# A two-block fp32 transformer kernel: row factors on ScalarE, a norm's scale and bias moved behind its mix, a 64-row matmul widened, first loads reordered

## The chip, the cores and the metric

The kernel runs on one core of one Trainium2 chip. The metric is the time on the device in microseconds, the median of three runs. A profile is one execution of its own, taken by the hardware profiler; its times are those of that execution. A core has TensorE (matmuls, written into PSUM), VectorE (DVE), ScalarE (ACT), GpSimd (POOL, which also issues some loads) and SyncE (SP, which issues most loads). Each engine takes its instructions in order and waits on semaphores.

## The reference, cut to what matters

512 tokens of width 1024 pass through two blocks of two layers each, all in fp32. The parts that the change touches:

```python
# first block, per layer: h = rms_norm(x); three branches on h @ w_in
def gmlp_branch(u, v, z, ln_g, ln_b, w_s, b_s):          # gating norm
    u = gelu(u)
    v = layer_norm(gelu(v), ln_g, ln_b)                  # scale and bias per column
    vc = v.reshape(bsz, seq // 128, 128, 4, 128)
    mixed = einsum("gpq,bnqgc->bnpgc", w_s, vc) + b_s.T[None, None, :, :, None]
    return u * mixed.reshape(bsz, seq, 512) * silu(z)

# delta net, chunks of tokens, both directions, 4 heads of 128:
lower = where(strict, einsum("nbhid,nbhjd->nbhij", kc * bc[..., None], kc) * decay, 0.0)
sol = triangular_solve(lower + eye, rhs, lower=True)     # then a scan over the chunks

# second block, first layer: attention with scores
s = einsum(q_nope, k_nope) + einsum(q_pe, k_pe)          # 128 + 64 (position) dims
p = softmax(s * scale)
```

## The kernel before, in words

Activations are kept with features on partitions. Every large product is made of three fp32r matmuls: an operand is split into a high part (ScalarE copy) and a low remainder (VectorE subtraction), and hi*hi, hi*lo and lo*hi are added up in PSUM. Weights come in blocks of 256 rows by up to 512 columns (`wload`, tile `wraw`, three buffers, SP's queue), are split by `wsplit` into `whi` and `wlo` and used by `gemm_it`, a generator that yields after each six matmuls or so. PSUM has eight banks, all from one pool (`s`).

**Order.** The Tile framework puts the instructions into one queue per engine, by the order of the program and by when it reckons them ready; `issue_after` holds an instruction behind another on its own engine. In the delta net, `rounds` and `spend` interleave generators: after each step of the delta net, a share of a "fill" generator (the gemms of the gates, of the gating norm's three segments `gu`, `gv`, `gz`, and of the retention's values) is emitted, so that TensorE has matmuls while VectorE works.

**Opening (lines 139 to 148, 275 to 391).** `x_load` issues the four 128-token tiles of x on SP, then `open_gemm` issues the weight blocks. `norm_halves` computes the squares on ScalarE (line 233, into PSUM), the root on GpSimd (241), the scaling on VectorE (287), transposes on TensorE (292), and from them the high and low parts times a gain (297, 298), first for tokens 0 to 255, then for the others. `weights` splits a weight block (356, 360). Line 374 is the matmul. The gain's load `g_b` is issued on ScalarE's queue.

**Delta net (`gdn`).** The four token chunks are worked on in two batches of two steps, each with both directions: four `front` generators, one `invert`, four `levels`, then `recur` for each step. `front` multiplies a mask by decays on GpSimd (1022), exponentiates on ScalarE (1028), masks again on GpSimd (1032), multiplies by the row factors `sM` on VectorE into `DM` (1035, one buffer), and from it and the keys' product in PSUM makes `Mall` (1037, twice) and `Mo` (1040). `values` transposes v into PSUM (996) and scales it. `invert` turns `Mall` around on VectorE (1056 to 1063), solves 16 rows in turn (1068, 1070), masks the result and its transpose into `tw` (one buffer; lines 1081 on VectorE for j=0, 1083 on ScalarE for j=1) and turns them into `ZZ[:, 0]` and `ZZ[:, 1]` (1085). `levels` starts with 64x64 matmuls of `Mall` and `ZZ[:, 1]` (1097); from the second pair on (1105, 1108) it uses `ZZ[:, 0]` as well.

**Gating norm (`gmlp`).** `ev_v` normalises a token tile (VectorE 647 to 651), then GpSimd multiplies by the scale (652) and adds the bias (653), rows spread over partitions. `mix_tokens` makes four matmuls with the transposed mixing weights `wsT` (659), VectorE adds `bs` (661), GpSimd multiplies by u times z (662).

**Attention of the second block (`mla`).** `head` gives five score terms: three for the 128 plain dims, and for the position dims `qpe` (high part of q in rows 0 to 63, low part in rows 64 to 127) with `khh` (high part of k twice), and the upper half of `qpe` with `kll` (low part of k, twice as well). Line 1377 is the score matmul, 8 heads by 4 token tiles.

## Time and profile before

| | us |
|---|---|
| median of three runs (2660.98 to 2662.34) | 2661.1 |
| the profiled execution | 2660.55 |
| its span, first to last instruction | 2658.8 |
| TensorE busy in it | 2583.6 |
| VectorE busy | 1416.0 |
| ScalarE busy | 1009.2 |
| GpSimd busy | 421.1 |

In the rows further down, the first number of a timeline row is the start in us from the span's start, the second how long it was busy, then engine, line, operation, tile written and tiles read, shape, count; in square brackets stands the idle time of the engine just before, and what ended it. Rows with a count above one cover several instructions in a row. TensorE's times are those of its pipeline: the distance from one matmul's start to the next says more than the length of one.

### The profile page before, as it was taken

How to read it: one execution, taken by the hardware profiler on the slowest of the kernel's cores; microseconds unless marked ns; L12 is line 12 of the kernel's file. 1: busy time of each engine (PE TensorE's matmuls, PEld its weight loads, DVE VectorE, ACT ScalarE, POOL GpSimd, SP SyncE). 2: the span in 40 equal slices, each digit the busy share in tenths (PEclk: the TensorE clock that was granted, in tenths of full speed). 3: DMA queues.
4: the chain of work that ended last, by engine and by line, in shares of the span. 5: the costliest groups of instructions: out<-in, count | busy, mean ns of one | idle time of the engine just before them, and what ended most of it. 6: DMA issues, size and time to landing. Idle time of an engine off the chain costs nothing.

```text
span 2658.8 us, 36067 instructions
## 1 busy us (share of the span) xinstructions
PE 2583.6 (97%) x14236; PEld 2150.5 (81%) x14236; DVE 1416.0 (53%) x2432; ACT 1009.2 (38%) x2163; POOL 421.1 (16%) x504
## 2 busy tenths in 40 slices
PE   8998999999999899999998999999999999999999
PEld 6777888888877788888787778888888788888887
DVE  4758565333675946533556764433344587443333
ACT  4433333223443233322446653322243575322221
POOL 3304211101131421110124430000002121000000
PEclk9999999999999999999999999999999999999999
DMA  5111132233411122234441112333335211233332
GB/s 157 58 57 40 42 101 64 95 104 129 126 56 57 40 70 72 71 95 141 134 120 32 37 64 88 101 93 102 91 120 161 88 48 56 88 89 101 103 95 87
DMA packets 117978, 231.03 MB, mean 87 GB/s; under 512 B 9584, under 2 KB 21488, under 8 KB 117808
## 3 DMA queue, kind: packets, MB, share of 16 engines
q1 hardware_dynamic: 113600, 221.28, 26.8%
q0 software_dynamic: 3024, 7.37, 1.2%
q8 instruction: 112, 1.84, 0.3%
q14 instruction: 58, 0.48, 0.1%
q10 hardware_dynamic: 1184, 0.07, 0.0%
HBM read 220.30 MB, written 8.39 MB: 86 GB/s over the span
## 4 chain that ended last, share of the span: by engine, by line
PE 61%; DVE 4%; POOL 2%; issue 1%; ACT 1%; POOLq 0%; DVEq 0%; ACTq 0%
PE s L536 49%; PE s L1377 3%; PE s L1421 2%; PE s L374 2%; PE s L1406 1%; PE s L1356 0%; DVE wlo L211 0%; PE s L267 0%; PE s L1097 0%; PE s L1105 0%; PE s L758 0%; PE s L1108 0%; POOL hqr L202 0%; DVE tmp L1068 0%; PE s L750 0%
## 5 line engine op out<-in xcount | busy, mean ns | idle before, releaser
L536 PE MATMUL s<-slot,whi 128*128 128x512 f32 x3200 | 1000.1, 393 | 0.0
L211 DVE TENSOR_TENSOR wlo<-wraw,whi 128x1024 fp32r<-128x1024 f32 (+4 forms) x378 | 455.9, 1207 | 788.4 <-ACT whi L210 787.9
L210 ACT ACTIVATE whi<-wraw 128x1024 fp32r<-128x1024 f32 (+4 forms) x378 | 384.5, 1018 | 935.8 <-PE s L536 876.1
L536 PE MATMUL s<-whi,slot 128*128 128x512 f32 (+2 forms) x2288 | 737.4, 391 | 0.4 <-DVE hqe L200 0.2
L536 PEld LDWEIGHTS s<-slot,whi 128*128 128x128 f32 x3200 | 598.7, 189 | 122.2
L536 PE MATMUL s<-slot,wlo 128*128 128x512 f32 x1600 | 625.9, 391 | 0.0
L536 PEld LDWEIGHTS s<-whi,slot 128*128 128x128 f32 x2288 | 427.3, 188 | 85.2 <-issue 3.9
L536 PE MATMUL s<-wlo,slot 128*128 128x512 f32 (+2 forms) x1144 | 439.3, 384 | 0.0
L536 PEld LDWEIGHTS s<-slot,wlo 128*128 128x128 f32 x1600 | 301.9, 189 | 63.4
L536 PEld LDWEIGHTS s<-wlo,slot 128*128 128x128 f32 x1144 | 215.3, 188 | 35.1
L241 POOL TENSOR_TENSOR rmsr<-rmse,mhalf 128x1 f32<-128x1 f32 x32 | 19.7, 618 | 563.0 <-DVE rmse L239 563.0
L1317 POOL TENSOR_TENSOR acc<-acc,pm 128x512 f32<-128x512 f32 x32 | 49.7, 1578 | 341.9 <-DVE pm L1313 225.9
L210 ACT ACTIVATE slot<-s 128x512 fp32r<-128x512 f32 (+2 forms) x144 | 75.1, 531 | 59.2 <-PE s L1406 40.5
L211 DVE TENSOR_TENSOR slot<-s,slot 128x512 fp32r<-128x512 f32 (+2 forms) x144 | 84.5, 592 | 24.4 <-ACT slot L210 23.9
L374 PE MATMUL s<-slot,whi 128*128 128x256 f32 (+1 forms) x384 | 88.4, 326 | 0.8 <-ACT slot L297 0.7
L1388 POOL TENSOR_TENSOR p<-p,a_ri 128x512 f32<-128x512 f32 (+1 forms) x48 | 43.9, 915 | 210.7 <-DVE a_ri L1384 182.2
L1382 ACT ACTIVATE p<-s,a_mx 128x512 f32<-128x512 f32 (+1 forms) x96 | 59.3, 619 | 39.8 <-DVE a_mx L1379 37.7
L374 PEld LDWEIGHTS s<-slot,whi 128*128 128x128 f32 x384 | 64.3, 194 | 6.8 <-ACT slot L297 1.4
L1379 DVE TENSOR_REDUCE a_mx<-s 128x1 f32<-128x512 f32 (+1 forms) x96 | 57.1, 595 | 22.1 <-PE s L1377 21.0
L1421 PE MATMUL s<-slot,slot 128*128 128x256 f32 x456 | 68.4, 292 | 0.4 <-DVE slot L211 0.4
L456 DVE TENSOR_TENSOR slot<-slot,s 128x512 f32<-128x512 f32 x64 | 42.5, 684 | 42.1 <-PE s L536 41.2
L1421 PEld LDWEIGHTS s<-slot,slot 128*128 128x128 f32 x456 | 59.7, 191 | 3.8 <-ACT slot L210 1.6
(402 smaller groups left out, 3187.4 us busy)
## 6 DMA issues: line engine op xcount, KB each, us to landing
wraw<-in_w_in_dram SPq DMA_DIRECT2D x88, 512.0 KB, 3.6
wraw<-in_w_gate_up_dram SPq DMA_DIRECT2D x64, 512.0 KB, 3.6
wraw<-in_w_gate_dram SPq DMA_DIRECT2D x48, 512.0 KB, 3.6
wraw<-in_w_out_dram SPq DMA_DIRECT2D x40, 512.0 KB, 3.8
wraw<-in_w_down_dram SPq DMA_DIRECT2D x40, 512.0 KB, 3.8
wraw<-in_w_branch_out_dram SPq DMA_DIRECT2D x24, 512.0 KB, 3.8
wraw<-in_w_gate_up_dram SPq DMA_DIRECT2D x32, 384.0 KB, 3.3
wraw<-in_w_mem_kv_dram SPq DMA_DIRECT2D x16, 512.0 KB, 3.7
```

Source lines behind the costliest of these rows:

```text
L210: nc.scalar.activation(hi, src, AF.Copy)
L211: return nc.vector.tensor_tensor(out=lo, in0=src, in1=hf, op=ALU.subtract)
L374: nc.tensor.matmul(pts[i][:wd, ts_], lhsT=l, rhs=r, start=(half == 0 and k0 == k == j == 0), stop=(k0 == KD - 2 and k == 1 and j == 2), sk ...
L456: nc.vector.tensor_tensor(out=self.x[t][:, cs], in0=self.x[t][:, cs], in1=p, op=ALU.add)
L536: nc.tensor.matmul(ov, lhsT=l, rhs=r, start=(kk == first and j == 0), stop=(k0 == final and k == n - 1 and j == 2))
L1317: nc.gpsimd.tensor_tensor(out=acc[i], in0=acc[i], in1=m, op=ALU.add)
L1377: nc.tensor.matmul(pt[:, :n], lhsT=l_[:, ts_], rhs=r_, start=(i == 0), stop=(i == len(q_terms) - 1))
L1379: nc.vector.tensor_reduce(out=mx, in_=pt[:, :n], axis=AX.X, op=ALU.max, negate=True)
L1382: nc.scalar.activation(p, pt[:, :n], AF.Exp, bias=mx, accum_out=sm)
L1388: nc.gpsimd.tensor_tensor(out=p, in0=p, in1=ri.to_broadcast([P, n]), op=ALU.mult)
L1406: nc.tensor.transpose(pp[:, k, :], p[:, k * P:(k + 1) * P], self.ident)
L1421: nc.tensor.matmul(po[:, hs], lhsT=l_, rhs=r_, start=(k == 0 and j == 0), stop=(k == nk - 1 and j == 2))
```

## The change

Six edits:

- `x_load`: at the first load, the weight blocks 0 and 2 of the first gemm are issued on SP after x[1], before x[2] and x[3]. `weights` takes them from there.
- `squares` and `norm_halves`: in the first norm, whose squares are not known from a layer before, the squares go to SBUF instead of PSUM, and the roots for tokens 256 to 511 come after the first half's four gain parts in the program.
- `gmlp`: scale and bias are read as columns. The bias, times the row sums of the mixing weights (a matmul with ones, `offsets`), is added into `bs` once a layer; the scale is applied with that sum after the mix, in four instructions on 128x128. The two GpSimd instructions per token tile fall away.
- `gdn`: the Exp of the decay rate is held behind the norm's last high part on ScalarE.
- `front`: DM is made by four ScalarE instructions, one a head. `invert`: ZZ[:, 1] is made first, on VectorE, then ZZ[:, 0], on ScalarE.
- `mla`: the fifth score term uses all 128 rows of `qpe` and `kll`; it adds the product of the low parts.

```diff
@@ -146,6 +146,8 @@
                 e.enter_context(self.tc.issue_after(self.last_w))
             for t in range(NT):
                 nc.sync.dma_start(out=self.x[t], in_=self.x_home[t])
+                if t == 1 and self.last_w is None:
+                    self.early = {k0: self.wload(self.a["w_in"][0], k0, 2, SEG["dk"], 512) for k0 in (0, 2)}
 
     def x_store(self):
         self.x_home = [self.dr.tile([P, DM], F32, tag=f"xh{t}", name=self.nm("xh")) for t in range(NT)]
@@ -225,12 +227,13 @@
         r = self.rsqrt_eps(ms, 1, "nr")
         nc.vector.scalar_tensor_tensor(out=out, in0=xt, scalar=r, in1=gain, op0=ALU.mult, op1=ALU.mult)
 
-    def squares(self, src):
+    def squares(self, src, junk=None):
 
         ms = self.sm([P, 2], "sq_ms")
         for c in range(2):
             s_ = src[:, c * 512:(c + 1) * 512]
-            self.nc.scalar.activation(self.ps(), s_, AF.Square, scale=float(DM) ** -0.5, accum_out=ms[:, c:c + 1])
+            o = self.ps() if junk is None else junk[:, c * 512:(c + 1) * 512]
+            self.nc.scalar.activation(o, s_, AF.Square, scale=float(DM) ** -0.5, accum_out=ms[:, c:c + 1])
         return ms
 
     def rms(self, ms):
@@ -281,7 +284,7 @@
         pts = {}
 
         def rms(t):
-            rs.append(self.rms(self.ms[t] if self.ms is not None else self.squares(self.x[t])))
+            rs.append(self.rms(self.ms[t] if self.ms is not None else self.squares(self.x[t], hs[t])))
 
         def scale(t):
             nc.vector.tensor_scalar(out=hs[t], in0=self.x[t], scalar1=rs[t], scalar2=None, op0=ALU.mult)
@@ -304,7 +307,9 @@
         rms(1)
         scale(0)
         yield
-        rms(2)
+        known = self.ms is not None
+        if known:
+            rms(2)
         scale(1)
         yield
         yield
@@ -314,9 +319,13 @@
         for k in range(4):
             turn(k, 1)
             part(k, A)
-            if k == 1:
+            if k == 1 and known:
                 rms(3)
                 scale(2)
+        if not known:
+            rms(2)
+            rms(3)
+            scale(2)
         scale(3)
         yield
         for t in (2, 3):
@@ -346,7 +355,7 @@
 
         def weights(k0):
             if k0 not in ws:
-                raw = self.wload(ap, k0, 2, c0, cw)
+                raw = self.early.pop(k0, None) or self.wload(ap, k0, 2, c0, cw)
                 hi = self.T(self.pw, [P, 2, 512], "whi", F32R, 3)
                 lo = self.T(self.pw, [P, 2, 512], "wlo", F32R, 3)
                 raw, h, w = raw[:, :, :cw], hi[:, :, :cw], lo[:, :, :cw]
@@ -615,8 +624,8 @@
     def gmlp(self, l, es, w_in, ya):
         tc, nc, a = self.tc, self.nc, self.a
         pool = es.enter_context(tc.tile_pool(name=f"gm{l}", bufs=1))
-        lng = self.rows(pool, a["gm_ln_g"][l], W, "lng")
-        lnb = self.rows(pool, a["gm_ln_b"][l], W, "lnb")
+        lng = self.cols(pool, a["gm_ln_g"][l], 4, "lng")
+        lnb = self.cols(pool, a["gm_ln_b"][l], 4, "lnb")
         bs = self.rows(pool, a["gm_b_s"][l].rearrange("g p -> (g p)"), W, "bs")
         ws = self.T(pool, [P, 4, P], "g2", F32, 2)
         self.load(ws, a["gm_w_s"][l].rearrange("g p q -> p g q"))
@@ -626,6 +635,17 @@
             nc.tensor.transpose(pt[:, g, :], ws[:, g, :], self.ident)
         nc.scalar.activation(wsT, pt, AF.Copy)
         uz = ya
+        add = bs.rearrange("p (g q) -> p g q", g=4)
+
+        def offsets():
+
+            pr = self.ps([P, 4, P])
+            nc.tensor.matmul(pr.rearrange("p g q -> p (g q)"), lhsT=self.ones, rhs=wsT.rearrange("p g q -> p (g q)"),
+                             start=True, stop=True)
+            for g in range(4):
+                nc.vector.scalar_tensor_tensor(out=add[:, g], in0=pr[:, g], scalar=lnb[:, g:g + 1], in1=add[:, g],
+                                               op0=ALU.mult, op1=ALU.add)
+
         spatial, vs = [], []
 
         def ev_u(i, p):
@@ -649,8 +669,6 @@
             nc.vector.bn_aggr(out=mv, in_=st)
             r = self.rsqrt_eps(mv[:, 1:2], 1, "g")
             nc.vector.tensor_scalar(out=v, in0=v, scalar1=mv[:, 0:1], scalar2=r, op0=ALU.subtract, op1=ALU.mult)
-            nc.gpsimd.tensor_tensor(out=v, in0=v, in1=lng, op=ALU.mult)
-            nc.gpsimd.tensor_tensor(out=v, in0=v, in1=lnb, op=ALU.add)
             spatial.append((t, v))
 
         def mix_tokens(t, v):
@@ -658,11 +676,14 @@
             for g in range(4):
                 nc.tensor.matmul(pm[:, g, :], lhsT=v[:, g * P:(g + 1) * P], rhs=wsT[:, g, :], start=True, stop=True)
             m = self.T(pool, [P, 4, P], "g2", F32, 2)
-            nc.vector.tensor_tensor(out=m, in0=pm, in1=bs.rearrange("p (g q) -> p g q", g=4), op=ALU.add)
+            for g in range(4):
+                nc.vector.scalar_tensor_tensor(out=m[:, g], in0=pm[:, g], scalar=lng[:, g:g + 1], in1=add[:, g],
+                                               op0=ALU.mult, op1=ALU.add)
             nc.gpsimd.tensor_tensor(out=ya[:, :, t * P:(t + 1) * P], in0=m, in1=uz[:, :, t * P:(t + 1) * P], op=ALU.mult)
 
         def work():
             yield from self.gemm_it(w_in, KD, SEG["gu"], 512, self.hT, "T", ev_u)
+            offsets()
             yield from self.gemm_it(w_in, KD, SEG["gv"], 512, self.hT, "N", ev_v)
             n = 0
             for _ in self.gemm_it(w_in, KD, SEG["gz"], 512, self.hT, "T", ev_z):
@@ -897,7 +918,8 @@
                 nc.scalar.activation(zb[:, :, d], ab[:, :, d, 1], AF.Tanh, scale=0.5)
             spl = self.softplus(pool, za.rearrange("p t d h -> p (t d h)"), 32, "dsp")
             ar = T([P, 8], "ar")
-            nc.scalar.activation(ar, alg, AF.Exp)
+            with tc.issue_after(self.normed_hi):
+                nc.scalar.activation(ar, alg, AF.Exp)
             nc.vector.scalar_tensor_tensor(out=g, in0=spl.rearrange("p (t d) -> p t d", t=NT), scalar=-1.0,
                                            in1=ar.unsqueeze(1).to_broadcast([P, NT, 8]), op0=ALU.mult, op1=ALU.mult)
             nc.vector.tensor_scalar(out=beta, in0=zb.rearrange("p t d h -> p t (d h)"), scalar1=1.0, scalar2=0.5,
@@ -1032,7 +1054,8 @@
             nc.gpsimd.tensor_tensor(out=D, in0=D, in1=incl, op=ALU.mult)
             yield
             DM_ = T([P, H, P], "DM", 1)
-            nc.vector.tensor_tensor(out=DM_, in0=D, in1=bh(sM[:, c, d]), op=ALU.mult)
+            for h in range(H):
+                nc.scalar.activation(DM_[:, h], D[:, h], AF.Identity, scale=sM[:, c, d, h:h + 1])
             for b in range(2):
                 nc.vector.tensor_tensor(out=Mall[B[b], d, step % 2], in0=pk[B[b], :, B[b]], in1=DM_[B[b], :, B[b]], op=ALU.mult)
             if step not in Mo:
@@ -1070,19 +1093,19 @@
                 nc.vector.tensor_reduce(out=Ya[:, :, i, 0:i], in_=pr, axis=AX.X, op=ALU.add, negate=True)
                 if i % 3 == 0:
                     yield
-            for j in range(2):
-                if j:
+            for n, j in enumerate((1, 0)):
+                if n:
                     W_.append(T([P, 2, 16, 32], "tw", 1))
                 for d in range(2):
                     src = (Ya if d == j else Yt)[:, d]
                     for e in range(2):
-                        o = W_[j][:, d, :, e * 16:e * 16 + 16]
-                        if j == 0:
+                        o = W_[n][:, d, :, e * 16:e * 16 + 16]
+                        if n == 0:
                             nc.vector.tensor_scalar(out=o, in0=src, scalar1=self.half[:, e:e + 1], scalar2=None, op0=ALU.mult)
                         else:
                             nc.scalar.activation(o, src, AF.Copy, scale=self.half[:, e:e + 1])
                 for d in range(2):
-                    nc.vector.transpose(mid(ZZ[:, j, d]), W_[j][:, d].rearrange("p k (c s) -> p k c s", c=4))
+                    nc.vector.transpose(mid(ZZ[:, j, d]), W_[n][:, d].rearrange("p k (c s) -> p k c s", c=4))
                 yield
 
         def levels(step, d, Mall, ZZ):
@@ -1718,7 +1741,7 @@
                     nc.tensor.transpose(pt[:, t * P:(t + 1) * P], pe_hl[t][:, h].rearrange("p e d -> p (e d)").bitcast(F32), self.ident)
                 qpe = T([P, 512], "qpe", 2, F32R)
                 nc.scalar.activation(qpe, pt, AF.Copy)
-                terms = self.three(qT, kT) + [(qpe, khh), (qpe[0:64], kll[0:64])]
+                terms = self.three(qT, kT) + [(qpe, khh), (qpe, kll)]
                 if h == 1 and g < 3:
                     started.append(g + 1)
                 return terms, lambda k: vh[:, k, h], lambda k: vl[:, k, h], 2 * g + h
```

## Rows read from the trace of the kernel before

**Rows 1.** Waits of TensorE, whole span: total us, times, longest us.

```profile
PE s L1097 <- DVE ZZ L1085: 21.5, 6, 6.9
...
PE s L996 <- DVE Mo L1040: 11.5, 2, 5.8
```

**Rows 2.** Timeline, first layer, fronts of the first batch.

```profile
107.67 5.44 DVE L1035 TENSOR_TENSOR DM<-slot,sM 128x512 f32<-128x512 f32 x1 [2.79 <-POOL slot L1032]
...
108.09 1.03 POOL L1022 TENSOR_TENSOR t<-tri,g 128x512 f32<-128x512 f32 x1
...
111.31 1.25 POOL L1032 TENSOR_TENSOR slot<-slot,tri 128x512 f32<-128x512 f32 x1
113.21 0.86 DVE L1037 TENSOR_TENSOR Mall<-s,DM 64x256 f32<-64x256 f32 x2
...
114.56 1.11 PE L996 MATMUL s<-ident,slot 128*128 128x128 f32 x4 [5.76 <-DVE Mo L1040]
```

**Rows 3.** Line 1035, ns min/median/max; timeline, four ScalarE products by row factors.

```profile
L1035 DVE TENSOR_TENSOR DM<-slot,sM x16: 673/692/5441, 107.7 to 871.3; 128x512 f32<-128x512 f32 x16
...
218.05 1.14 ACT L1163 ACTIVATE t<-s,ee 128x128 f32<-128x128 f32 x4 [0.73 <-PE s L1160]
```

**Rows 4.** Windows: us, busy us (count) of PE, PEld, DVE, ACT, POOL; clock, DMA.

```profile
114.00:116.00 2.00, 1.44 (x6) 1.35 (x7) 1.77 (x5) 0.00 (x0) 0.00 (x0) 0.50 0.00 0
...
156.00:158.00 2.00, 2.00 (x29) 1.83 (x28) 2.00 (x4) 0.11 (x1) 0.00 (x0) 0.50 0.04 8
...
266.00:268.00 2.00, 2.00 (x16) 1.25 (x16) 1.34 (x3) 0.51 (x1) 0.76 (x1) 0.50 0.76 244
...
1484.00:1612.00 128.00, 127.99 (x690) 101.64 (x688) 87.40 (x208) 72.82 (x225) 40.06 (x62) 1.00 0.18 56
```

**Rows 5.** Timeline, first layer, end of the first invert.

```profile
149.78 1.31 DVE L1081 TENSOR_SCALAR tw<-Y,half 128x256 f32<-128x256 f32 x4
...
153.03 2.13 ACT L1083 ACTIVATE tw<-Y,half 128x256 f32<-128x256 f32 x4 [9.60 <-DVE ZZ L1085]
...
155.52 1.79 PE L1097 MATMUL s<-ZZ,Mall 64*64 64x64 f32 x28 [3.45 <-DVE ZZ L1085]
```

**Rows 6.** Timeline, first layer, second invert: a hold, and its end.

```profile
228.80 1.29 POOL L652 TENSOR_TENSOR slot<-slot,lng 128x512 f32<-128x512 f32 x1 [0.66 <-DVE slot L651]
228.86 1.37 DVE L1068 TENSOR_TENSOR tmp<-L,Y 128x72 f32<-128x72 f32 x1
...
255.03 2.50 DVE L1081 TENSOR_SCALAR tw<-Y,half 128x256 f32<-128x256 f32 x4
...
261.98 0.70 PE L1097 MATMUL s<-ZZ,Mall 64*64 64x64 f32 x8 [6.92 <-DVE ZZ L1085]
```

**Rows 7.** Timeline: TensorE's fp32 128x512 product; VectorE's four 128x128 with PSUM.

```profile
202.08 1.02 PE L1025 MATMUL s<-t,tri 128*128 128x512 f32 x2
...
295.92 1.13 DVE L1141 SCALAR_TENSOR_TENSOR u<-s,ee,slot 128x128 f32<-128x128 f32 x4 [4.86 <-PE s L1138]
```

**Rows 8.** Timeline of TensorE in the attention, one score's end.

```profile
1510.88 0.40 PE L1377 MATMUL s<-khh,qpe 128*128 128x512 f32 x1
1511.21 0.49 PE L1377 MATMUL s<-kll,qpe 64*128 64x512 f32 x1
1511.63 0.50 PE L536 MATMUL s<-whi,slot 128*128 128x512 f32 x1
1511.97 0.40 PE L536 MATMUL s<-wlo,slot 128*128 128x512 f32 x1
```

**Rows 9.** Timeline of the opening.

```profile
7.56 0.60 ACT L233 ACTIVATE s<-slot 128x512 f32<-128x512 f32 x1 [0.24 <-DMA slot<-in_x_dram]
...
11.48 0.84 ACT L297 ACTIVATE slot<-s,g_b 128x256 fp32r<-128x256 f32 x2 [1.76 <-DMA g_b<-in_norm_g_dram]
...
13.53 2.02 ACT L356 ACTIVATE whi<-wraw 128x1024 fp32r<-128x1024 f32 x2
...
14.66 2.07 PE L374 MATMUL s<-slot,whi 128*128 128x256 f32 x8
```

## The prediction

> **What bounds the kernel now.** I read the page's busy shares first: TensorE is busy for 2583.6 of the span's 2658.8 us (the table above), so nearly all of the run is matmul, and only two things can move the end: fewer or cheaper matmuls, or less of the 75 us in which TensorE stands still. The reader is to see next, in the waits of TensorE, where it stands: the largest are its level matmuls behind ZZ, 21.5 us in six waits, three a layer, and the transposes of the values behind Mo, 11.5 us, one wait of 5.8 us a layer [rows 1]. Both lie in the delta net, in both layers alike. [...] Last, the timeline of each wait, since a wait's name is only its last link.
>
> **Row factors on ScalarE (line 1035).** Sixteen VectorE products (eight a layer) become sixteen times four ScalarE products. Alone one takes 0.69 us, but the longest took 5.44 [rows 2, 3]: it starts at 107.67 and ends 0.5 us after the last of four back-to-back GpSimd products, 108.09 to 112.56. Mall and Mo follow it, and TensorE, whose values transpose waits for their PSUM bank, idles 5.76 us. Two operands from SBUF beside GpSimd is what marks the long one; Mall, with one operand in PSUM, keeps its 0.43.
> Moved, the product starts at about the same time (ScalarE has nothing else to do there), takes some 1.15 us as the nearest ScalarE row has it for four 128x128 [rows 3], then two Mall and Mo at 0.43 each: 107.7 + 1.15 + 1.3 + 0.15 for two handovers = 110.3 instead of 114.56. That is 4.3 us of idle less, and with 1.5 us of idle the clock should not fall: at 0.50 TensorE worked about 3.2 us from 114.56, of which 1.6 were lost [rows 2, 4]. Against that, the one DM buffer now passes between two engines: each further front takes 1.15 + 1.3 = 2.5 us instead of 0.69 + 1.3 = 2.0, so the third front's bank comes free at 115.3, while TensorE would want it at 114.3. I give back 1.0 and a little: 4.7 us a layer (bounds 2 and 5.9).
> In the second batch nothing holds VectorE that long, and the handover is pure cost: 0.5 us in each of four fronts, with VectorE free for its other work meanwhile. I take 0.5 us lost a layer (bounds 0 and 3).
> [...]
>
> **Order in invert (lines 1073 to 1085).** The first level matmul needs only ZZ[:, 1]. Before, ZZ[:, 0] came first: four VectorE products from 149.78, then two transposes, only at 153.03 (one tw buffer) ScalarE's four products, then the other transposes; TensorE stands from 152.07 to 155.52 [rows 5]. From 151.09 to 153.03 are 1.0 for one transpose, so afterwards the half that TensorE wants first is ready after 1.3 + 1.0 us, at about 152.0, for the same number of instructions. The other half arrives where it did, around 155.4, and TensorE needs it only after four level groups and a filler, about 3.4 us later: 155.5. So 3.45 us of idle go, and with them the half clock: about 3.1 us of work at 0.50 [rows 4], 1.5 us lost. VectorE's chain before this must move up with TensorE's 4.7; it loses three products of 0.69 there, so it should. 4.7 us a layer (bounds 3 and 5).
> In the second batch VectorE reaches the same point at 255.03, TensorE runs dry at 255.06 and waits 6.92 us, to 261.98 [rows 6]. By order alone it would start at 255.03 + 2.3 (3.5 if the products stay at the 2.50 of the row), a wait of 2.3 to 3.5; if VectorE gains that much before, the wait is zero. The half clock lasts to 268 [rows 4]: about 5.6 us of work at half rate, 2.8 lost. Together 6.9 + 2.8 = 9.7.
>
> **Scale and bias of the gating norm.** That lead comes from here. The two GpSimd products per token tile go (eight instructions of about 1.3 us a layer), and they held VectorE: one of its small products starts 0.06 us after the GpSimd one and ends 0.14 after it, 1.37 us long [rows 6], some 1.1 of them the hold. If half of the eight do that, VectorE gains 4.4 us, an estimate. It pays: each mix becomes four instructions of 0.28 (four on 128x128 with an operand in PSUM: 1.13) in place of one on 128x512 at 0.69 [rows 3, 7], 0.45 more, of which two come before 255; and the offsets, four more, about 1.1, in a stretch where VectorE waits for TensorE. 4.4 - 0.9 + 2.8 for the four row products - 2 of idling between handovers = 4.3, more than the 2.3 to 3.5 wanted. So 9.5 us a layer (bounds 4.5 and 9.7). TensorE pays for the offsets' matmul: 1.02 us at most, as the 128x512 product of the same type [rows 7]; I take 0.9. The two column loads take GpSimd's queue some 0.4 us longer each, 60 us before they are read: nothing.
>
> **Sum of the delta net:** 4.7 + 4.7 - 0.5 + 9.5 - 0.9 = 17.5 a layer, 35.0 for two.
>
> **Position term over 128 rows (line 1721).** The scores' fifth matmul uses 64 rows. From the fourth's start to the fifth's are 0.33 us, from there 0.42, and the next step 0.34, where the ones before are 0.23 apart [rows 8]: 1.09 against 0.69. The 128-row form should keep the pace: 0.40 us, 32 times. From 1484 to 1612, where 26 of the 32 lie, TensorE is busy for 127.99 of 128 us and VectorE for 87 [rows 4], so there every saved step is the end's; before, the chain that ended last leaves TensorE several times. 26 x 0.40 = 10.4 us (bounds 5 and 12.8).
>
> **First loads.** TensorE's first weight matmul is at 14.66, after ScalarE's two weight copies began at 13.53 (2.02 for both), which stood behind the gain parts, which waited for the gain's load until 11.48 [rows 9]. The third load of x was awaited until 7.56 and those behind it land one after another, so the two weight blocks, now third and fourth, land near 7.6 and, an estimate, 1.5 us on, and ScalarE, idle until the gain, can copy them there. The gain's load is not moved. Then matmuls start near 12.2, 2.4 us earlier; the squares of x[2] and x[3] come after the parts and must be through when 48 matmuls are. I take 2.5 (bounds 3.5, and -2.4 if ScalarE keeps to the order as written, where the copies come behind the parts and then four squares of 0.6 [rows 9]). Squares written to SBUF and the later Exp of the decay rate are priced at nothing: in both layers TensorE has work at that Exp; cover gone, a few tenths.
>
> **The sum** is made against the profiled execution, 2660.55 us, which is 0.55 under the median of the runs: 2660.55 - 35.0 - 10.4 - 2.5 = 2612.65.
>
> **The rivals.**
> *The handover takes the wait's place*, 2633: DM passes through one buffer eight times a layer, and if ScalarE's Exps stand ahead of the products in the second batch, its fronts end 3 us later. Then a layer gains 2 in the first front, 4 in the first invert, loses 3, gains 5 in the second invert, loses 0.9: 7.1, twice, plus 12.9. For it: a serial chain of 10 us; against: VectorE has other work in the gaps. 18 in 100.
> *The attention is not TensorE's alone*, 2618: VectorE's maximum and splits take over once scores come faster, and half of the 10.4 goes. Against: from 1484 on VectorE is idle for a third of the time [rows 4]. 10 in 100.
> *GpSimd is not what held the product*, 2622: it starts before the first of the four GpSimd products, 107.67 against 108.09, and still ends behind them all [rows 2]; if it was something else, and that holds ScalarE alike, the 4.7 a layer are gone: 2612.65 + 9.4. Against: its end follows theirs closely. 5 in 100. [...]
> *Slower, 2712:* ScalarE works in order. If a row product is queued behind a weight copy that waits for a buffer which TensorE frees, and TensorE waits for that product's Mo, each front stalls; at 4 us in sixteen fronts 64 us come on, and only 12.9 are gained elsewhere. It decides from (12.9 + 5.3) / 16 = 1.1 us a front. Against: in the program's order the products of the first fronts stand ahead of the copies of the third weight block. 4 in 100.
> *It doesn't do what it says*, 2661: the order of instructions comes out otherwise and eats the gains. 4 in 100.
>
> **How the numbers follow.** The forecast, 2613 with a range of its own of 2605 to 2622, has 59 in 100. A measurement of this kernel can tell about 0.2%, 5.3 us, from no change. Faster by more: 59 + 18 + 10 + 5 = 92; within: 4; slower: 4. The range must reach to the first rival, 2633 and a little, and on the other side to the sum of the better bounds, 2660.55 - 2 x (5.9 + 5.0 + 9.7 - 0.9) - 12.8 - 3.5 = 2605, with some us below it for the smaller waits that I left standing: 2597 to 2636.
>
> **What would show it.** TensorE's wait behind Mo falls to about 1.5 us a layer, the waits behind ZZ to under 3 in total, and no 2 us stretch of the delta net has the clock at 0.50. Row products on ScalarE take 1.1 to 1.2 us for four. No 64-row score matmul is left, and the steps of a score are 0.23 apart. The first weight matmul is near 12.2. I am wrong if a wait on the row products or on ScalarE's Exps appears in the fronts, if the clock still falls, or if ScalarE takes the copies late in the opening.

## The result and the profile after

The median of four runs is 2628.1 us (2626.9 to 2630.6); beside it on the same chip the kernel before took 2661.6. The ratio is 0.9875 (95% interval 0.9858 to 0.9892): 33.5 us gained, of the 47.9 forecast. The profiled execution of after took 2630.55 us, 2.4 over the median, with a span of 2628.8, so the two traces lie 30.0 apart: 17.9 of the forecast sum are missing in them, and the account below has to say where. In the medians 14.4 are missing; the other 3.5 belong to the two executions that were profiled.

What TensorE waits for now, with total us, times and longest us; it answers to [rows 1]:

```profile
PE s L1120 <- DVE g L680: 5.6, 2, 2.8
...
PE s L1053 <- ACT slot L1050: 4.9, 2, 2.4
...
PE s L1128 <- DVE Q L1123: 4.1, 5, 1.4
...
PE s L1120 <- DVE ZZ L1108: 0.8, 3, 0.4
```

The 21.5 us behind ZZ are 0.8, and the 11.5 behind Mo are gone. In their place stand three waits that the forecast's sum did not have: behind a mix of the gating norm (line 680), behind an Exp (1050), and behind Q (1123), the product that VectorE masks between two level matmuls.

How far after is ahead, from TensorE's rows at the same places of the program. First after, then before:

```profile
202.14 1.16 PE L1161 MATMUL s<-S,slot 128*128 128x128 f32 x8 [0.63 <-ACT slot L1050]
...
414.05 0.87 PE L793 MATMUL s<-ident,ron 128*128 128x128 f32 x3 [2.25 <-DVE ron L788]
...
1059.49 0.87 PE L793 MATMUL s<-ident,ron 128*128 128x128 f32 x3 [2.25 <-DVE ron L788]
...
1266.20 0.33 PE L270 MATMUL s<-ident,slot 128*128 128x128 f32 x1 [1.09 <-DVE slot L256]
...
1374.73 0.41 PE L1612 MATMUL s<-ident,ckn 128*128 128x128 f32 x2 [1.27 <-DVE nre L202]
...
2087.30 0.30 PE L1379 MATMUL s<-ident,slot 128*128 128x128 f32 x1 [1.12 <-DVE de L202]
```

```profile
211.88 1.16 PE L1138 MATMUL s<-S,slot 128*128 128x128 f32 x8 [0.89 <-DVE Mo L1040]
...
429.73 0.88 PE L772 MATMUL s<-ident,ron 128*128 128x128 f32 x3 [2.23 <-DVE ron L767]
...
1085.06 0.88 PE L772 MATMUL s<-ident,ron 128*128 128x128 f32 x3 [2.23 <-DVE ron L767]
...
1290.17 0.33 PE L267 MATMUL s<-ident,slot 128*128 128x128 f32 x1 [1.09 <-DVE slot L253]
...
1396.84 0.41 PE L1589 MATMUL s<-ident,ckn 128*128 128x128 f32 x2 [1.28 <-DVE nre L200]
...
2118.43 0.30 PE L1356 MATMUL s<-ident,slot 128*128 128x128 f32 x1 [1.12 <-DVE de L200]
```

| place | ahead, us |
|---|---|
| first layer, second batch | 9.7 |
| first layer, last wait of the retention | 15.7 |
| second layer, last wait of the retention | 25.6 |
| norm after the first block | 24.0 |
| before the attention with scores | 22.1 |
| after it | 31.1 |
| end of the span | 30.0 |

The lead grows where the change is, and shrinks four times where nothing was changed: 15.7 to 14.1 behind the first retention (the second layer's first weight matmul starts at 657.06, before at 671.14), 25.6 to 24.0, 24.0 to 22.1, 31.1 to 30.0. That is 6.2 us. Some 0.3 of it is a longer wait in front of the norm before the scores (2.00 us, before 1.71). The rows of the retention's wait tell the rest: TensorE waits for `ron` 2.23 us before and 2.25 after, and then, in windows of 2 us (busy us and count of PE, PEld, DVE, ACT, POOL; granted clock; DMA), first after, then before:

```profile
414.00:416.00 2.00, 1.95 (x8) 1.42 (x9) 2.00 (x6) 0.75 (x2) 0.47 (x1) 0.82 0.00 0
...
416.00:418.00 2.00, 2.00 (x7) 1.51 (x6) 1.85 (x3) 0.63 (x2) 2.00 (x2) 0.50 0.00 0
...
418.00:420.00 2.00, 2.00 (x9) 1.65 (x8) 2.00 (x2) 0.63 (x1) 0.51 (x1) 0.83 0.00 0
```

```profile
432.00:434.00 2.00, 2.00 (x11) 1.64 (x10) 1.85 (x2) 0.64 (x1) 2.00 (x2) 1.00 0.00 0
```

The same wait in front of the same work is followed by a granted clock of 0.50 (a half clock, below) in one trace and not in the other. It costs 1.95 x 0.18 + 2.0 x 0.50 + 2.0 x 0.17 = 1.7 us, and the lead falls by 1.6.

The places of the change, in after's timeline. The first fronts, timeline of ScalarE, then of TensorE, which answers to [rows 2, 3] (the Exp is line 1050, the row products 1058):

```profile
104.90 0.99 ACT L1058 ACTIVATE DM<-slot,sM 128x128 f32<-128x128 f32 x3 [4.01 <-POOL slot L1054]
...
105.80 0.57 ACT L1050 ACTIVATE slot<-s 128x512 f32<-128x512 f32 x1
...
111.57 1.28 ACT L1058 ACTIVATE DM<-slot,sM 128x128 f32<-128x128 f32 x4 [2.19 <-DVE Mo L1063]
...
106.42 1.16 PE L1053 MATMUL s<-slot 128*128 128x128 f32 x8 [2.43 <-ACT slot L1050]
```

No 5.44 us product, no wait behind Mo, and the clock stays at 1.00 from 104 to 116. But ScalarE takes the Exp of the second front only between the row products of the first, which themselves stood until 104.90 behind GpSimd's mask, and TensorE waits 2.43 us for the PSUM bank that the Exp frees. Four row products take 1.28.

The second invert, timeline of VectorE, then of TensorE, which answers to [rows 6] and, with the window behind it, to the 266:268 row of [rows 4]:

```profile
241.86 1.98 DVE L1108 STREAM_TRANSPOSE ZZ<-tw 128x512 f32<-128x512 f32 x2
...
243.69 1.04 DVE L680 SCALAR_TENSOR_TENSOR g<-s,lng,bs 128x128 f32<-128x128 f32 x4
...
247.03 2.33 DVE L213 TENSOR_TENSOR wlo<-wraw,whi 128x1024 fp32r<-128x1024 f32 x2
...
249.28 1.12 DVE L680 SCALAR_TENSOR_TENSOR g<-s,lng,bs 128x128 f32<-128x128 f32 x4
...
244.33 1.15 PE L1120 MATMUL s<-ZZ,Mall 64*64 64x64 f32 x32
...
250.46 0.68 PE L1120 MATMUL s<-ZZ,Mall 64*64 64x64 f32 x16 [2.77 <-DVE g L680]
```

The window in which its clock stands at 0.50 throughout:

```profile
252.00:254.00 2.00, 2.00 (x28) 1.78 (x25) 1.97 (x4) 0.00 (x0) 0.00 (x0) 0.50 0.39 147
```

TensorE starts its level matmuls at 244.33 without a wait, where it had waited 6.92. It then stands 2.77 us behind a mix, and the clock falls to 0.50. VectorE hardly idles there (0.17 us): behind the half that TensorE wanted come a mix, the other half, two weight remainders (2.33) and another mix (1.12).

The end of a score (TensorE) and the opening (ScalarE, then TensorE), which answer to [rows 8, 9]:

```profile
1484.81 0.40 PE L1400 MATMUL s<-khh,qpe 128*128 128x512 f32 x1
...
1485.04 0.39 PE L1400 MATMUL s<-kll,qpe 128*128 128x512 f32 x1
...
1485.27 0.39 PE L545 MATMUL s<-whi,slot 128*128 128x512 f32 x1
...
9.67 1.06 ACT L365 ACTIVATE whi<-wraw 128x1024 fp32r<-128x1024 f32 x1 [0.53 <-DMA wraw<-in_w_in_dram]
...
11.08 1.57 ACT L300 ACTIVATE slot<-s,g_b 128x256 fp32r<-128x256 f32 x4 [0.35 <-DMA g_b<-in_norm_g_dram]
...
11.60 1.22 PE L383 MATMUL s<-slot,whi 128*128 128x256 f32 x4 [0.88 <-ACT slot L300]
```

The five terms and what follows are 0.23 apart, and the first weight matmul is at 11.60 instead of 14.66.

### The profile page after: what moved, and what is told of

It is laid out like the page before. It is cut to its first block, busy times and chain, and to the rows that moved or that the text cites. A ratio compares the mean times of both kernels' runs of the same rounds, so it can differ in the third digit from the quotient of the medians.

```text
span 2628.8 us, 36135 instructions
## 1 busy us (share of the span) xinstructions
PE 2573.5 (98%) x14240; PEld 2153.0 (82%) x14240; DVE 1384.6 (53%) x2448; ACT 1027.4 (39%) x2227; POOL 400.3 (15%) x488
## 4 chain that ended last, share of the span: by engine, by line
PE 84%; DVE 8%; POOL 3%; ACT 3%; issue 2%; DMA 0%; ACTq 0%; POOLq 0%; DVEq 0%
PE s L545 67%; PE s L383 4%; PE s L1400 2%; PE s L1444 2%; DVE wlo L213 1%; PE s L1429 1%; PE s L1128 1%; DVE tmp L1091 1%; PE s L1131 1%; PE s L779 1%; PE s L771 0%; POOL hqr L204 0%; PE s L1379 0%; PE s L295 0%; DVE Y L1093 0%
```

## The experiments

All medians below are of at least four runs, each set beside runs of the kernel before of its own (2661.6 to 2662.6 in the median). The traces are of one execution of each kernel.

| kernel | median, us | ratio to before (95%) |
|---|---|---|
| before + position term | 2653.0 | 0.9966 (0.9954 to 0.9979) |
| before + order in invert | 2650.7 | 0.9960 (0.9947 to 0.9972) |
| before + row factors | 2656.4 | 0.9977 (0.9968 to 0.9986) |
| before + gating norm | 2656.2 | 0.9978 (0.9969 to 0.9987) |
| after | 2628.1 | 0.9875 (0.9858 to 0.9892) |
| after, row factors on VectorE in four | 2642.8 | 0.9929 (0.9916 to 0.9941) |
| after, row products behind the Exps, both batches | 2627.2 | 0.9872 (0.9858 to 0.9885) |
| the same, first batch alone | 2622.8 | 0.9853 (0.9840 to 0.9867) |
| after, level products between the halves | 2645.9 | 0.9940 (0.9927 to 0.9954) |
| after, idle transposes in a wait | 2625.9 | 0.9867 (0.9854 to 0.9881) |
| before, GpSimd thinned out | 2654.4 | 0.9972 (0.9961 to 0.9982) |
| after, gate products on VectorE | 2621.5 | 0.9849 (0.9836 to 0.9863) |
| three edits together | 2618.0 | 0.9834 (0.9820 to 0.9847) |

**The four parts, each alone on the kernel before.** The edits are hunks of the change; their core:

```diff
-                terms = self.three(qT, kT) + [(qpe, khh), (qpe[0:64], kll[0:64])]
+                terms = self.three(qT, kT) + [(qpe, khh), (qpe, kll)]
```

> The kernel before with the position term over 128 rows alone. The prediction's step: 26 of 32 scores at 0.40 us, 10.4 us, so 2651. From the changed kernel's trace, where the lead of 22.1 us at the first scores has become 31.1 at 2004 us: 9.0 us, so 2653. Rival (the attention is not TensorE's alone, half of it goes): 2656. If the 0.40 us belong to something else than the 64 rows: 2661.6, no change.

It took 9.1 us off, as the trace of after has it (22.1 to 31.1). The forecast 10.4 is missed by what VectorE takes for the remainders of the softmax: TensorE now waits 0.49 and 1.05 us behind them in the middle of the attention, in this kernel as in after. Followed matmul by matmul, after's lead falls by 1.0 and 1.4 us at these two places. It also rises by 0.5 at the start of the attention, before the scores gain anything, where the clock stood at 0.50 for longer in the trace of before; that half microsecond is not the position term's.

```diff
-            for j in range(2):
+            for n, j in enumerate((1, 0)):
```

> The kernel before with the other order in invert alone. The prediction's step: 4.7 us in the first invert of a layer; in the second, by order alone, the wait of 6.92 falls to 2.3 to 3.5, some 4 us with no lead of VectorE: 8.7 a layer, 17.4 for two, so 2644. Rival: what VectorE has queued behind the half that TensorE wants first (the other half, a weight remainder of 1.2 us) delays Q, and TensorE waits there as it does in the changed kernel (1.39 in the first invert, 2.77 in the second): 3.3 + 1.5 a layer, so 2652. If the second invert can't use the order at all: 2652 with the 6.92 still there.

It took 11.4 off, 17.4 were forecast. The second invert of the first layer, timeline of TensorE:

```profile
256.57 2.01 PE L1097 MATMUL s<-ZZ,Mall 64*64 64x64 f32 x32 [3.58 <-DVE ZZ L1085]
...
263.00 0.68 PE L1097 MATMUL s<-ZZ,Mall 64*64 64x64 f32 x16 [1.35 <-DVE g L661]
```

The wait of 6.92 is 3.58, just over the 2.3 to 3.5 forecast, and a new one of 1.35 (0.50 in the second layer) stands behind a mix; in the first invert 1.45 behind Q. So the rival was right: VectorE has more queued than the half that was moved. The clock took a part too: it fell behind the second layer's retention (1.6 us), which it does not in before, and stayed low longer behind the unchanged wait for Mo in the first layer (3.0 lost by the windows, before 1.6). The same window of 2 us behind that wait, first in this kernel, then in the one before:

```profile
118.00:120.00 2.00, 2.00 (x6) 1.54 (x5) 1.94 (x4) 0.00 (x0) 0.00 (x0) 0.50 0.00 0
```

```profile
118.00:120.00 2.00, 2.00 (x9) 1.43 (x8) 1.94 (x4) 0.73 (x1) 0.00 (x0) 1.00 0.00 0
```

Up to 151 us, every engine has the same instructions in the same order in both kernels. So this difference of 1.3 us is not the edit's: it lies between two executions. The medians show it as well: four executions of this kernel took 2650.1 to 2651.0 us, the fifth 2655.4, with the lowest mean clock of the five (0.991, against 0.992 to 0.994).

```diff
-            nc.vector.tensor_tensor(out=DM_, in0=D, in1=bh(sM[:, c, d]), op=ALU.mult)
+            for h in range(H):
+                nc.scalar.activation(DM_[:, h], D[:, h], AF.Identity, scale=sM[:, c, d, h:h + 1])
```

> The kernel before with the row factors on ScalarE alone. The prediction's step: 4.7 in the first front less 0.5 in the second batch, 8.4 for two layers, so 2653. Theory from the changed kernel's trace: the wait of 5.76 behind Mo goes with its half clock, and one of 2.43 comes behind an Exp that stands behind row products on ScalarE: 4.9 a layer if the handover costs nothing later, so 2652. Rival (the handover takes the wait's place, 3 us lost in the second batch): 2658.

It took 5.7 off. At the retention's last wait the lead is 429.73 - 424.55 = 5.2 us, and behind it the clock falls (1.6, which before did not lose), as it does behind the second layer's. So the part itself is worth some 4.9 a layer in this trace, as the trace of after led to expect, and two half clocks take 3.2 back. The handover does not take the wait's place: the wait for ZZ in the second invert grows from 6.92 to 7.84, at most 0.9 of the 3 that the rival names.

```diff
-            nc.gpsimd.tensor_tensor(out=v, in0=v, in1=lng, op=ALU.mult)
-            nc.gpsimd.tensor_tensor(out=v, in0=v, in1=lnb, op=ALU.add)
...
-            nc.vector.tensor_tensor(out=m, in0=pm, in1=bs.rearrange("p (g q) -> p g q", g=4), op=ALU.add)
+            for g in range(4):
+                nc.vector.scalar_tensor_tensor(out=m[:, g], in0=pm[:, g], scalar=lng[:, g:g + 1], in1=add[:, g],
+                                               op0=ALU.mult, op1=ALU.add)
```

> The kernel before with the gating norm's scale and bias on mixed tokens alone. The prediction's step: VectorE is freed of holds worth 4.4 us, pays 0.9 for the mixes, so the wait of 6.92 in the second invert shrinks by 3.5; TensorE pays 0.9 for the offsets: 2.6 a layer, so 2656. Rival (the GpSimd products cost VectorE nothing that counts): 0.9 for the offsets and 0.9 for the mixes a layer are lost, so 2665.

It took 5.9 off. The wait of 6.92 in the second invert became 2.81:

```profile
260.19 1.93 PE L1109 MATMUL s<-ZZ,Mall 64*64 64x64 f32 x32 [2.81 <-DVE ZZ L1097]
```

That is 4.1 less, where 3.5 were forecast, but only 1.8 of it is ZZ coming earlier (260.19 for 261.98). The other 2.3 are TensorE's own: it runs dry at 257.38 instead of 255.06, 0.9 later by the offsets' matmul and 1.3 by a half clock that lasted longer behind the first layer's wait for Mo, ahead of anything that the edit touches there. The number came out near the forecast, the split did not.

The four add up to 9.1 + 11.4 + 5.7 + 5.9 = 32.1, each known to some 2 to 3 us by its interval; with 2.8 of the opening (its last weight matmul starts at 38.38, before at 41.14; not run alone) that is 34.9, against 33.5 for all at once. So no large help of the parts for each other shows; one of a few us could not be seen. The forecast had let them help: its 9.5 for the second invert needed order and lead together to bring the wait to nothing.

**What held the long product.** After, with the row factors back on VectorE, in four instructions:

```diff
-                nc.scalar.activation(DM_[:, h], D[:, h], AF.Identity, scale=sM[:, c, d, h:h + 1])
+                nc.vector.tensor_scalar(out=DM_[:, h], in0=D[:, h], scalar1=sM[:, c, d, h:h + 1], scalar2=None, op0=ALU.mult)
```

> The changed kernel with the row factors back on VectorE, as four products by a scalar column each, which have one 128x128 operand from SBUF where the product of before had two of 128x512. Theory that two large SBUF operands beside GpSimd make the long product: four short ones of about 0.28 us each, no hold, no row products in front of the Exps, so the wait of 2.43 us behind the Exp goes in both layers, and with it the half clock that follows it in the second: 2628.1 - 4.9 - 1.5, about 2622, less what VectorE's 1.1 us in sixteen fronts cost. Rival (GpSimd holds VectorE whatever its operands): the first of the four products lasts until GpSimd's instructions end, some 4 us, TensorE waits for Mo again: about 2634.

Before, with less on GpSimd in the first fronts:

```diff
-            nc.gpsimd.tensor_tensor(out=R, in0=incl, in1=bh(g4[:, c, d]), op=ALU.mult)
+            with ExitStack() as e:
+                if step > 1:
+                    e.enter_context(tc.issue_after(masked[3]))
+                (nc.gpsimd if step > 1 else nc.vector).tensor_tensor(out=R, in0=incl, in1=bh(g4[:, c, d]), op=ALU.mult)
```

> The kernel before, row factors on VectorE as there, with GpSimd thinned out in the first fronts: the four products of the decay gates of the first batch are VectorE's, and those of the second batch stand behind the last masked decay product on GpSimd. Theory (VectorE's row product lasts 5.44 us because GpSimd's instructions follow one another without a gap): GpSimd has only the masked products there, each behind an Exp and so apart, and the first row product ends in the first gap, within 2.5 us; TensorE's wait behind Mo (5.76) falls under 2, with the half clock after it in both layers: 2661.7 - 2 x (4 + 1.6), about 2650. Rival (not GpSimd, but the product itself or its operands): it still takes 5.4, 2661.7 or a little more.

Timelines of the first fronts, VectorE and then GpSimd: first the kernel with four products, then the thinned one:

```profile
103.99 5.55 DVE L1058 TENSOR_SCALAR DM<-slot,sM 128x128 f32<-128x128 f32 x4 [2.80 <-POOL slot L1054]
...
103.87 0.55 POOL L1141 MEMSET slot<- 64x256 f32 x2
...
107.61 1.25 POOL L1054 TENSOR_TENSOR slot<-slot,tri 128x512 f32<-128x512 f32 x1
```

```profile
106.84 1.75 DVE L1039 TENSOR_TENSOR DM<-slot,sM 128x512 f32<-128x512 f32 x1 [1.16 <-POOL slot L1036]
...
104.53 5.19 POOL L1036 TENSOR_TENSOR slot<-slot,tri 128x512 f32<-128x512 f32 x3 [1.89 <-ACT slot L1032]
```

Four products with one operand of a single head are held as long as the one with two: 5.55 us, of which the first instruction takes 4.98 (the shortest of them is 0.24, the median 0.28), until GpSimd's train of back-to-back instructions ends at 108.86. TensorE waits 5.88 behind Mo again, and the kernel loses 14.7 us. That is more than the rival's price (2634): in the second batch, where VectorE now makes these products too, new waits behind Mo come on (5.4 us in all). So it does not take two large operands, as the prediction had thought. With the gate products out of the train, the same product as before takes 1.75, TensorE's wait behind Mo falls from 5.76 to 0.90, and 7.2 us are gained, less than forecast because the wait in the first invert grows (4.12 for 3.45) and the clock stays at 0.50 for longer behind it. That rules the third rival out: GpSimd held the product. Not why, though: here three of GpSimd's products also follow without a gap (2.28, 1.26 and 1.69 us), and the row product, started 0.07 us after the second of them, got in where the third begins, which it delayed; in the kernel before it did not get in at four such joints.

The prediction held against GpSimd as the cause that the product starts at 107.67, ahead of the four GpSimd products from 108.09. It overlooked a row of the kernel before:

```profile
107.57 0.55 POOL L1118 MEMSET slot<- 64x256 f32 x2
```

Two GpSimd memsets run from 107.57, and in the kernel with four products they start 0.12 us before the held one. So GpSimd's train had begun ahead of the product in both. The memsets end at 108.12 and the product lasted to 113.11; why it was not let in behind them is not shown.

**The Exps and the row products.** After, with the row products held behind the latest Exp on ScalarE:

```diff
+            with tc.issue_after(exps[-1]):
+                for h in range(H):
+                    nc.scalar.activation(DM_[:, h], D[:, h], AF.Identity, scale=sM[:, c, d, h:h + 1])
```

> The changed kernel with each front's row products held behind the latest Exp on ScalarE, so that no Exp stands behind a row product. Theory (ScalarE works in order; TensorE waits 2.43 us in each layer's first front for a PSUM bank that an Exp frees, and the Exp stands behind a product that waits for GpSimd): that wait goes, and in the second layer the half clock after it, 1.5: 2628.1 - 6.4, about 2622. The row products start no later, since the first waits for GpSimd until 104.9 us anyway. Rival (the bank is only the next thing: Mo comes late, and TensorE waits there as long): 2628, with a wait behind Mo.

Timeline of the first layer: ScalarE's fourth row products of the second batch, then TensorE's first level matmul in the second invert:

```profile
209.64 1.28 ACT L1060 ACTIVATE DM<-slot,sM 128x128 f32<-128x128 f32 x4 [2.07 <-DVE Mo L1065]
...
246.63 1.97 PE L1122 MATMUL s<-ZZ,Mall 64*64 64x64 f32 x32 [6.46 <-DVE ZZ L1110]
```

The wait of 2.43 went, in both layers. But the fourth row products of the second batch start at 209.64 instead of 205.79, the last 2.07 us of it waiting for VectorE, and TensorE waits 6.46 in the second invert where it waited 2.77. Only 1 us is left, no more than the runs scatter: what the first rival of the prediction described, fronts of the second batch that end 3 us late, came about when the order was turned round. So the same edit for the first batch alone:

```diff
+                if step < 2:
+                    e.enter_context(tc.issue_after(exps[-1]))
```

> The changed kernel with the row products held behind the latest Exp in the first batch of a layer alone. Theory from the run that held them in both batches: there the wait of 2.43 in the first front went, and the second batch, whose four row products then all stood behind the fourth Exp, ended 3.7 us later and gave it back. Held in the first batch alone, the 2.4 stay gained, in both layers, with 1.5 of half clock in the second: 2628.1 - 6.3, about 2622. Rival (VectorE sets the second invert whatever precedes it, so that TensorE only waits longer there): 2627, with a wait of some 5 us in the second invert.

2622.8, as expected: 5.3 gained. The other way to the same end takes the cause away, GpSimd's queue in front of the first mask (the edit of the thinned kernel, on after):

```diff
-            nc.gpsimd.tensor_tensor(out=R, in0=incl, in1=bh(g4[:, c, d]), op=ALU.mult)
+            (nc.gpsimd if step > 1 else nc.vector).tensor_tensor(out=R, in0=incl, in1=bh(g4[:, c, d]), op=ALU.mult)
```

> The changed kernel with the first batch's products of the decay gates on VectorE, which is idle there, and those of the second batch held on GpSimd behind the last masked product of the first. Theory (the first row product waits until 104.9 us for a masked product that stands in GpSimd's queue behind four gate products, while its Exp ended at 100.9): it starts some 2.5 us earlier, so the Exps behind it too, and TensorE's wait of 2.43 goes in both layers: 2628.1 - 6.3, about 2622. Rival (the gain is waited off in the second invert, or the second batch's gate products come late): 2627 or more.

The first front of the first layer, timeline of ScalarE, then of TensorE:

```profile
102.86 0.99 ACT L1062 ACTIVATE DM<-slot,sM 128x128 f32<-128x128 f32 x3 [2.39 <-POOL slot L1058]
...
104.38 1.16 PE L1057 MATMUL s<-slot 128*128 128x128 f32 x8 [1.04 <-ACT slot L1054]
```

The first row products (ScalarE) start at 102.86 instead of 104.90, TensorE's wait is 1.04 instead of 2.43, the Q waits of 1.39 in the first inverts are down to 0.26 (to 0.23 in the run just above), and the median is 2621.5.

**Order between the halves.** After, with the first level products issued between the two halves of invert:

```diff
+                if n == 0:
+                    for lv in lvs:
+                        next(lv)
                 yield
```

> The changed kernel with the first level products issued between the two halves of invert, so that VectorE has their Q ahead of the other half's transposes, the weight remainders and the mix. Theory (what is left of the waits in the inverts is VectorE's order: 1.39 us in a layer's first invert behind a weight remainder, 2.77 in the second behind remainders and a mix, and about 1.6 of half clock behind that): 5.7 a layer at most, so about 2617. Rival (VectorE is the bound there, whatever the order: the waits only pass from Q to ZZ): 2628.

TensorE's first level matmuls in the first invert of the first layer:

```profile
145.61 3.71 PE L1123 MATMUL s<-ZZ,Mall 64*64 64x64 f32 x64 [4.65 <-DVE ZZ L1108]
```

A miss, 17.8 us slower than after, by neither theory: the edit moved TensorE's level matmuls too, ahead of the gemm that had filled the time until ZZ was there, and TensorE waits some 4.7 and 7.6 us for ZZ in the two inverts of each layer. An order written for VectorE was one for TensorE as well.

**The clock behind unchanged waits.** After, with work for TensorE in the retention's last wait:

```diff
+            if h == 3:
+                for t in range(14):
+                    nc.tensor.transpose(pt[:, (t % 4) * P:(t % 4 + 1) * P], self.ident, self.ident)
```

> The changed kernel with 14 more transposes of the identity, whose result nothing reads, ahead of the retention's last transposes in each layer, where TensorE waits 2.25 us for VectorE. Theory (the half clock that follows these waits in the changed kernel and not in the kernel before comes from the idle time, and costs 1.6 a layer): TensorE has work in the wait, the clock stays, 2628.1 - 3.2, about 2625, with the waits themselves no shorter in sum. Rival (the fall of the clock has another cause): 2628, with half clock at both places.

TensorE's timeline in the first layer's wait, and the window behind it:

```profile
412.67 1.69 PE L794 MATMUL s<-ident 128*128 128x128 f32 x14
...
414.98 1.28 PE L796 MATMUL s<-ident,ron 128*128 128x128 f32 x4 [0.62 <-DVE ron L788]
```

```profile
414.00:416.00 2.00, 1.38 (x8) 0.60 (x7) 1.49 (x5) 1.08 (x2) 0.48 (x1) 1.00 0.00 0
```

The 14 transposes fill 1.69 us of the wait, 0.62 remain, and the clock stays at 1.00, in both layers. The median is 2.2 us lower, which alone would not be clear of the scatter. All the kernels run together tell more. Whether a window with the clock at 0.50 stands behind four waits of unchanged work ("-" where none does; retention waits are 2.23 to 2.26 us long, those of the grouped queries 1.12):

| kernel | retention 1 | retention 2 | norm before the scores | grouped queries |
|---|---|---|---|---|
| before | - | - | - (1.71) | - |
| after | 0.50 | 0.50 | 0.50 (2.00) | 0.50 |
| position term | - | - | - (1.71) | - |
| order in invert | - | 0.50 | - (1.71) | - |
| row factors | 0.50 | 0.50 | - (1.71) | - |
| gating norm | 0.50 | - | 0.50 (1.99) | - |
| four on VectorE | - | 0.50 | 0.50 (2.00) | 0.50 |
| behind the Exps, both | 0.50 | 0.50 | - (1.71) | 0.50 |
| behind the Exps, first | 0.50 | 0.50 | 0.50 (2.01) | 0.50 |
| between the halves | - | - | 0.50 (2.02) | 0.50 |
| GpSimd thinned | - | - | - (1.72) | 0.50 |
| gate products on VectorE | 0.50 | 0.50 | - (1.72) | - |
| idle transposes | filled: - | filled: - | - (2.00) | 0.50 |
| three together | filled: - | filled: - | - (1.71) | 0.50 |

Of the 24 unfilled retention waits, all alike to 0.03 us, 13 are followed by the lower level. It comes in some traces and not in others, in kernels whose edits lie hundreds of us earlier. Whether it is the edit's shift or only the execution that decides is not shown, with one trace of each kernel; the pair of windows under the order in invert shows that the execution alone can. The wait in front of the norm is not quite the same everywhere, some 1.7 us in eight traces and 2.0 in six. The profiled execution of before happened to lose nothing at the four places.

That the transposes keep the clock up rests on four waits in two traces, and in four of the other twelve traces neither retention wait is followed by the lower level. The other executions support it: with the transposes the mean granted clock is 0.997 in three of four (0.995 in the fourth), without them 0.994 to 0.995 in all four.

**Together.** Gate products on VectorE, row products behind the Exps in the first batch, idle transposes:

```diff
+                (nc.gpsimd if step > 1 else nc.vector).tensor_tensor(out=R, in0=incl, in1=bh(g4[:, c, d]), op=ALU.mult)
...
+                if step < 2:
+                    e.enter_context(tc.issue_after(exps[-1]))
...
+            if h == 3:
+                for t in range(14):
```

> Three edits together on the changed kernel: the first batch's decay gate products on VectorE and the second batch's behind the last masked product, the first batch's row products behind the latest Exp, and 14 idle transposes of the identity in the retention's last wait of each layer. Theory: from 2621.5 of the first edit, the 1.04 us that TensorE still waits behind an Exp in each layer's first front go by the second, 2 us, and the two half clocks of 1.6 behind the retention's waits by the third, 3.2 less the 0.6 by which the idle transposes overrun: about 2617. Rival (VectorE or the second invert takes the 2 us back, and the clock falls at other places instead): 2620 to 2621.

2618.0, 10.1 under the changed kernel, where about 2617 was expected. From what TensorE still waits for:

```profile
PE s L1131 <- DVE g L680: 5.6, 2, 2.8
```

The 2.8 us behind the mix in each second invert are untouched by all of this.

## Why the prediction was right and where it was wrong

The direction and the range held (2597 to 2636), the own range of the forecast (2605 to 2622) did not, and 2613.0 was 15 us too low. That the range held is in part luck: its upper end was set for the first rival, which did not come about in this order, and the time lay so high by a queue and a clock that no rival named. By its steps, in us of the two traces:

- **First loads,** 2.5 forecast, 2.8 measured, by the way described: ScalarE copied the weights at 8.08 and 9.67, before the gain came.
- **Position term,** 10.4 forecast, 9.0 measured, 0.5 of them the clock's. Each score gained its 0.40; the cover of TensorE was not quite complete, since two waits of 1.5 us in all behind the remainders of the softmax appeared inside the stretch that the prediction had read as TensorE's alone.
- **Row factors,** 4.7 - 0.5 a layer forecast, some 4.9 in the trace of it alone. The size was right and the way partly wrong: of "wrong if a wait on ScalarE's Exps appears" the wait came, 2.43 us, where the prediction had put 1.5 behind Mo. It let the row product start freely at 107.7 because ScalarE "has nothing else to do there"; the Exps of the next two fronts were queued behind it. In the second layer the clock fell behind that wait (1.5). That it would not fall behind 1.5 us of idle was an estimate: behind the 1.12 us of the grouped queries it fell in eight of the fourteen traces. The row products took 1.28 for four, not 1.15: 0.59 more than one on VectorE. The handover's rival was priced about right, but did not happen in this order of ScalarE's queue.
- **Gating norm,** 3.5 of lead had been worked out; alone it took 4.1 from the wait, 1.8 of them by an earlier ZZ and the rest by a later TensorE.
- **First invert,** 4.7 forecast. The 3.45 went and with them the half clock, but 1.39 came back behind Q, where a weight remainder stands ahead.
- **Second invert,** 9.5 forecast, and this is the term that failed. The wait behind ZZ did go to nothing as worked out (order and lead exceeded what was wanted), but the step stopped there. What is late next was not asked: VectorE's queue behind the wanted half, 1.04 of a mix, 2.2 for the other half, 2.33 of remainders, 1.12 of a mix, before the first Q. 2.77 of wait and 1.6 of half clock a layer remain, 8.7 for two where 0.4 had been left. In two layers the delta net brought (15.7 - 2.8) + (25.6 - 14.1) = 24.4 instead of 35.0.
- **What no step had:** 6.2 us handed back at waits that the change does not touch, some 5.9 of them by the clock. In runs alone it shows as well (two half clocks with the row factors). The sum treated the clock of unchanged stretches as fixed. Whether the change brought these losses or only the profiled execution, these traces cannot tell; the profiled execution of after was the slowest of its four.

The account of the two traces closes: 10.6 short in the delta net, 1.4 in the attention, 6.2 at the unchanged waits, 0.3 better in the opening, 17.9 in all. Two signs named beforehand failed accordingly: a 2 us stretch of the delta net at 0.50 remains (252 to 254), and the Exp wait came.

Open: why VectorE is let in at some joints of GpSimd's train and not at others; whether the 2.77 us go when the mix and the remainders are out of VectorE's way, since they are read from its queue here and no run took them out; and whether Q could pass the remainders and the mix in the second invert without moving TensorE's own order, which was tried only in the form that failed.

## What to carry to other kernels

Where a stall is taken away by reordering a queue, list everything that stands in that queue up to the next thing the waiting engine needs, and price the whole list, not the item that was moved. When two edits shorten the same wait, subtract them from it together, and then from what comes up behind it. In a kernel whose matmul engine is nearly always busy, short waits elsewhere can have a clock cost that comes and goes from trace to trace, here 1.6 us each: compare two kernels there by several executions, not by one trace of each. Fourteen idle transposes in such a wait kept the clock at 1.00 in all four places where they were tried.

## What the hardware showed that was not expected

- The lower clock level follows a wait of 2.25 us about every other time (13 of 24), with equal work on both sides of it, and costs 1.6 to 1.7 us each time. Two kernels with the same instructions up to 151 us differ by 1.3 us behind the same wait for Mo (5.8 us), so the execution has a part in it. With 14 idle transposes in the wait the clock was 1.00 in all four places tried.
- A VectorE instruction with one 128x128 operand from SBUF and one scalar column was held to the end of GpSimd's train, 4.98 us in all; one with two 128x512 operands took 5.44.
- GpSimd is held by VectorE as well: with the gate products on VectorE, the first mask, started 0.07 us after a weight remainder, takes 2.27 us instead of 1.27:

```profile
100.48 1.22 DVE L213 TENSOR_TENSOR wlo<-wraw,whi 128x1024 fp32r<-128x1024 f32 x1
...
100.55 2.27 POOL L1058 TENSOR_TENSOR slot<-slot,tri 128x512 f32<-128x512 f32 x1 [1.88 <-ACT slot L1054]
```
